# Attention of a hybrid encoder layer: scores of both head pairs and a neighbour's values in one cluster over four PSUM banks

## The chip, the cores and the metric

The kernel runs on one core of one Trainium2 chip. The number is the device time of one launch in microseconds (us). Of a core's engines five matter: TensorE multiplies (in the profile PE, its weight loads PEld), VectorE (DVE), ScalarE (ACT) and GpSimd (POOL) work on elements, and the sync engine (SP) issues most DMAs. TensorE takes its products in the order of the program, and writes them to PSUM, which has eight banks of 512 fp32 columns.

## The reference

One step of a streaming encoder: 2048 prompt positions and 8 x 16 sample positions, model width 1024, two layers. Each layer computes one wide projection of the normed input, two mixers side by side, an output projection, and a gated embedding:

```
u = rms_norm(h) @ w_in ;  qa,ka,va,ga,qb,kb,vb,gb,ab = split(u)
A = window attention(qa, ka, va)   8 heads of 64, 2 key heads, with sinks
    s = q k^T / 8 over the own chunk of 64 keys and the two before (192 keys)
    m = max(max(s), sink) ; pr = exp(s - m) ; den = sum(pr) + exp(sink - m)
    o = (pr / den) v
B = gated linear attention(qb, kb, vb, gates)   4 heads, state 64 x 128 handed on
h = h + [A * silu(ga) ; head_norm(B) * silu(gb)] @ w_out
h = h + sigmoid(rms_norm(h) @ w_pg) * (p @ w_pe)
```

## The kernel before

**Tiles and groups.** The 2176 positions are 17 tiles of 128: 16 of the prompt and one of the sample. `GROUPS` cuts them into groups of 3, 4, 4, 3 and 3 tiles; the last one holds two prompt tiles and the sample tile. For each layer and group `phase_in` makes the projections and both mixers, and `phase_out` the output projection and the gated embedding.

**Big products.** Weights are split into a high and a low part by ACT and DVE (`w_split`), and `mm3` makes three fp32r products for each of 8 blocks of 128 rows: 24 products a unit, over 512 columns or as many as the group has positions (384 or 512). `unit_a` and `unit_b` are such units. They run on the array as one 128*128 tile.

**Small products.** Attention and GLA are fp32 products on parts of the array. Scores use 64 rows (one key head) by 128 columns, two heads' groups side by side; value products use 128 rows by 64 columns for the two full key blocks and 64 by 64 for the halves; GLA scores use 64 by 32. A profile row shows that as 64\*128, 128\*64 and so on, and each fp32 product as two rows. `chain` (L121) strings the products of one cluster together, so that no big product is put between them. `wait_for` adds a wait on the last of them.

**What sets the order.** `pump` (L276) steps generators in the background, in two lanes (`lanes=2`); the units of big products call it behind themselves, those of `vb` and `gb` also in their middle. Each `yield` ends a step. Then a scheduler places the instructions of each engine by estimated times.

**Attention of a prompt tile** (`attn_prompt`, L627). For each of the two head pairs `hp`: four score products into the two banks of `pair("s")`, `softmax` (L581: DVE takes the maximum, ACT four exponentials, DVE scales P), a step later six transposes of P to PSUM, copied by ACT (`ptf`) and DVE (`pth`). When both pairs are through and the gates `ga` are made, the value products go to the two banks of `pair("o")`, and `gate_mix` multiplies them by the gates. A tile's scores of the second pair come one or more steps after the first, with big products between.

**GLA.** `gla_a` makes exponentials and the GLA scores (`at`, `ke`), `gla_prompt` the outputs, the state and the normed output `on`, which `gla_out` transposes. The list of jobs puts `gla_a(0)` in front of the last attention tile; `later` holds the GLA jobs until the projections for them are made. `gla_sample` (group 4 only) makes the state products of the sample from `km` (POOL); `km` and `on` come from the same two buffers (tag `on`).

Of the kernel before, what the change touches and what calls it, by code (L numbers as in the profile page):

```python
# [8 lines left out]
F32 = mybir.dt.float32  # L9
# [37 lines left out]
def hybrid_step(ctx: ExitStack, tc: tile.TileContext, a: dict, o: dict):  # L47
# [84 lines left out]

    def pt(shape):
# [312 lines left out]

    def unit_a(xt, w, m, s0, sn, ps=None, gate=None, ks=(0, KD), end=False):
        c = slice(m * 128, m * 128 + 128)
        mm3(ps, gate=gate, first=ks[0] == 0, last=ks[1] == KD, after=freed(w, 1, ks[0]) if end else None,
            sides=[(w(0, k, c), w(1, k, c), xt[k // 4][:, k % 4, 0, s0:s0 + sn], xt[k // 4][:, k % 4, 1, s0:s0 + sn])  # L450
                   for k in range(*ks)])
        return ps


    def phase_in(l, gi, ip, xn, mslot, S_in):
# [19 lines left out]
        def is_sample(t):  # L475
            return t == NP
# [103 lines left out]
        banks_as("p")  # L580
        done = dict(attn=0, ga=False, S=S_in, g2={}, seq=0, scores=0, qk=False)  # L581
        lock = set()

        def softmax(ps, P, nsink4, wd_of):

# [3 lines left out]
            if wd_of is None:  # L589
                V.tensor_reduce(out=mv, in_=ps, axis=AX.X, op=ALU.max)  # L590
            else:
                for c in range(2):
                    V.tensor_reduce(out=mv[:, :, c], in_=ps[:, :, c, :wd_of[c]], axis=AX.X, op=ALU.max)
            V.scalar_tensor_tensor(out=mv, in0=mv, scalar=-0.125, in1=nsink4, op0=ALU.mult, op1=ALU.min)  # L594
            V.tensor_tensor(out=den[:, 1].rearrange("p (i c) -> p i c", c=2), in0=mv, in1=nsink4, op=ALU.subtract)
            for e in range(4):
                wd = ps.shape[3] if wd_of is None else wd_of[e % 2]
                p0 = 0 if wd_of is None else 128 - 64 * (e % 2)
                A.activation(out=P[:, e, p0:p0 + wd], in_=ps[:, e // 2, e % 2, :wd], func=ACTF.Exp, scale=0.125,  # L599
                             bias=mx[:, e:e + 1], accum_out=den[:, 0, e:e + 1])  # L600
            A.activation(out=den[:, 1], in_=den[:, 1], func=ACTF.Exp)
# [4 lines left out]
            for c in range(2):  # L606
# [21 lines left out]
        def attn_prompt(ti):  # L628
# [60 lines left out]
            done["attn"] += 1  # L689

        def attn_sample(ti):
            ckT = ip.tile([128, 8, 128], F32, tag="E", name="ckT", bufs=2)
# [60 lines left out]
        def later(f):  # L753
            while not done["qk"]:
                yield
            yield from f()
# [3 lines left out]
        order = list(range(nt))  # L760
        jobs = [attn_sample(ti) if is_sample(t) else attn_prompt(ti) for ti, t in aorder]
        if not is_sample(tiles[-1]):
# [10 lines left out]
        for b in range(2):  # L773
            w = w_get(l, gi, f"ga{b}")
            for m in range(2):
                for si, (s0, sn) in enumerate(subs):
                    w_ahead(1, (m + 1 + Z["wah"]) / 2)
                    ps = unit_a(xt, w, m, s0, sn, pm(sn), end=m == 1)
                    sg = sga[:, 2 * b + m, s0:s0 + sn]
# [3 lines left out]
                    if late:  # L783
                        continue
                    pump(Z["pga"])
        done["ga"] = True


        for b, nm in enumerate(("qb", "kb")):
            w = w_get(l, gi, nm)  # L790
            for m in range(2):
                for si, (s0, sn) in enumerate(subs):
                    w_ahead(1, (m + 1 + Z["wah"]) / 2)
                    ps = unit_a(xt, w, m, s0, sn, pm(sn), end=m == 1)
                    dst = qkb[:, b, s0 // TT:(s0 + sn) // TT, m, :]
# [69 lines left out]
        def gla_scores(ti, E):  # L865
# [124 lines left out]
        def gla_sample(ti, sgb):  # L990
# [418 lines left out]
```

## Time and profile before

| | us |
|---|---|
| median of 3 runs (2299.15 to 2301.09) | 2299.72 |
| the profiled execution | 2299.65 |
| its span, first to last instruction | 2297.9 |
| TensorE busy, of the span | 2260.0 (98%) |
| DVE, ACT, POOL busy | 1510.8, 1187.7, 649.6 |

Matmuls are pipelined, and a row's duration reaches from the start of a product to its end, so that rows overlap: the distance between two starts is what a product takes from the stream. The granted clock of TensorE is full (0.995 over the span).

### The profile page before, as it was taken

Reading aid. Unit: us, or ns where it says so; the run is one execution under the profiler, and the core shown is the slowest. Engines: PE = TensorE matmul, PEld = TensorE weight load, DVE = VectorE, ACT = ScalarE, POOL = GpSimd, SP = SyncE. Lnnn points to the kernel's source line nnn. Section 1 sums busy time; section 2 is a strip of 40 time slices with the busy share of each in tenths; the row PEclk is TensorE's granted clock in tenths of the full one; section 3 lists DMA queues with packets and bytes.
Section 4 is the critical chain, followed back from the end, with each engine's and each line's share of the span. In section 5 each row is a group of like instructions: output and inputs, shape, how many; then the busy total and the mean of one; then the engine's idle time right before and its main releaser. Section 6 shows DMA issues by size and latency. Waiting matters only on the chain.

```text
span 2297.9 us, 40325 instructions
## 1 busy us (share of the span) xinstructions
PE 2260.0 (98%) x14814; PEld 1949.3 (85%) x14814; DVE 1510.8 (66%) x3119; ACT 1187.7 (52%) x2802; POOL 649.6 (28%) x771
## 2 busy tenths in 40 slices
PE   8999999999999999999999999999999999999999
PEld 7889877887788889987988998778877888799889
DVE  7767656766567666765776776557665676676655
ACT  6556444654455545644665564445544455565443
POOL 3124212342223221422332241214412142223222
PEclk8999999999999999999999999999999999999999
DMA  5744423434243535553565544234431545365443
GB/s 170 266 150 141 166 87 125 140 111 174 65 157 119 195 107 176 172 194 121 184 208 196 171 133 156 100 122 138 142 142 57 160 126 206 97 188 194 157 137 102
DMA packets 151590, 341.81 MB, mean 149 GB/s; under 512 B 16688, under 2 KB 42672, under 8 KB 138592
## 3 DMA queue, kind: packets, MB, share of 16 engines
q1 hardware_dynamic: 150704, 338.34, 44.8%
q8 instruction: 117, 1.92, 0.3%
q10 hardware_dynamic: 688, 0.88, 0.1%
q14 instruction: 81, 0.66, 0.1%
HBM read 297.35 MB, written 41.68 MB: 148 GB/s over the span
## 4 chain that ended last, share of the span: by engine, by line
PE 84%; ACT 4%; DVE 4%; DMA 4%; issue 3%; POOL 2%; ACTq 0%; DVEq 0%; POOLq 0%; SPq 0%
PE mm L421 15%; PE mm L419 15%; PE mm L420 15%; PE pw L419 9%; PE pw L421 9%; PE pw L420 9%; PE o L131 3%; DMA raw<-in_w_pe_dram 2%; PE s L131 2%; DVE w L96 2%; PE s L125 2%; PE o L125 1%; ACT gsq L914 1%; ACT w L234 1%; PE t L131 1%
## 5 line engine op out<-in xcount | busy, mean ns | idle before, releaser
L96 DVE TENSOR_TENSOR w<-raw,w 128x512 fp32r<-128x512 f32 (+1 forms) x640 | 464.5, 753 | 153.0 <-ACT w L234 151.4
L234 ACT ACTIVATE w<-raw 128x512 fp32r<-128x512 f32 (+1 forms) x640 | 375.4, 627 | 219.3 <-DMA raw<-in_w_pe_dram 60.2
L96 POOL TENSOR_TENSOR ot<-gth,hst 128x384 f32<-128x384 f32 (+1 forms) x79 | 101.7, 1291 | 285.6 <-DVE gth L1208 261.4
L419 PE MATMUL mm<-B,w 128*128 128x384 f32 (+1 forms) x440 | 159.3, 362 | 2.1 <-DVE yq L489 1.5
L421 PE MATMUL mm<-B,w 128*128 128x384 f32 (+1 forms) x440 | 160.2, 364 | 0.0
L420 PE MATMUL mm<-B,w 128*128 128x384 f32 (+1 forms) x440 | 158.8, 361 | 0.0
L419 PE MATMUL pw<-mix,w 128*128 128x384 f32 (+1 forms) x424 | 152.6, 360 | 0.0
L421 PE MATMUL pw<-mix,w 128*128 128x384 f32 (+1 forms) x424 | 151.1, 356 | 0.0
L420 PE MATMUL pw<-mix,w 128*128 128x384 f32 (+1 forms) x424 | 151.0, 356 | 0.0
L420 PE MATMUL mm<-A,w 128*128 128x384 f32 (+1 forms) x408 | 147.9, 363 | 0.0
L419 PE MATMUL mm<-A,w 128*128 128x384 f32 (+1 forms) x408 | 147.4, 361 | 0.0
L421 PE MATMUL mm<-A,w 128*128 128x384 f32 (+1 forms) x408 | 147.4, 362 | 0.0
L96 POOL TENSOR_TENSOR acc<-sq,acc 128x384 f32<-128x384 f32 (+1 forms) x60 | 73.9, 1231 | 258.7 <-ACT sq L350 243.7
L599 ACT ACTIVATE P<-s,mx 128x192 f32<-128x192 f32 (+3 forms) x272 | 108.6, 412 | 71.6 <-DVE mx L594 58.7
L419 PE MATMUL mm<-w,B 128*128 128x512 f32 (+1 forms) x360 | 138.6, 385 | 0.0
L419 PE MATMUL mm<-w,A 128*128 128x512 f32 (+1 forms) x360 | 138.5, 385 | 0.0
L420 PE MATMUL mm<-w,B 128*128 128x512 f32 (+1 forms) x360 | 138.0, 383 | 0.0
L420 PE MATMUL mm<-w,A 128*128 128x512 f32 (+1 forms) x360 | 137.6, 382 | 0.0
L421 PE MATMUL mm<-w,A 128*128 128x512 f32 (+1 forms) x360 | 137.3, 382 | 0.0
L421 PE MATMUL mm<-w,B 128*128 128x512 f32 (+1 forms) x360 | 137.1, 382 | 0.0
L96 POOL TENSOR_TENSOR mix<-ga_t,mix 128x512 fp32r<-128x512 f32 x34 | 44.0, 1295 | 262.9 <-ACT mix L625 262.9
L1205 ACT ACTIVATE gth<-gth 128x384 f32<-128x384 f32 (+2 forms) x81 | 45.1, 560 | 126.0 <-DVE gth L1204 125.7
(325 smaller groups left out, 6337.7 us busy)
## 6 DMA issues: line engine op xcount, KB each, us to landing
raw<-in_w_in_dram SPq DMA_DIRECT2D x240, 256.0 KB, 3.1
raw<-in_w_out_dram SPq DMA_DIRECT2D x160, 256.0 KB, 3.1
raw<-in_w_pg_dram SPq DMA_DIRECT2D x160, 256.0 KB, 3.0
w<-k0vb SPq DMA_DIRECT2D x16, 1024.0 KB, 4.8
w<-k1vb SPq DMA_DIRECT2D x16, 1024.0 KB, 4.8
raw<-in_w_in_dram SPq DMA_DIRECT2D x40, 272.0 KB, 3.0
raw<-in_w_pe_dram SPq DMA_DIRECT2D x40, 256.0 KB, 3.5
w<-k0ga SPq DMA_DIRECT2D x8, 1024.0 KB, 5.4
```

What stands on the lines that cost most here:

```text
L96: (eng or G).tensor_tensor(out=out, in0=in0, in1=in1, op=op1)
L125: prev[0] = PE.matmul(**kw).ins
L131: prev[0] = PE.matmul(**kw).ins
L234: A.activation(out=hi, in_=r, func=ACTF.Copy)
L419: PE.matmul(out=out, lhsT=sh, rhs=mh, start=first and i == 0, stop=False)
L420: PE.matmul(out=out, lhsT=sh, rhs=ml, start=False, stop=False)
L421: lastmm[0] = PE.matmul(out=out, lhsT=sl, rhs=mh, start=False, stop=last and i == n).ins
L599: A.activation(out=P[:, e, p0:p0 + wd], in_=ps[:, e // 2, e % 2, :wd], func=ACTF.Exp, scale=0.125, bias=mx[:, e:e + 1], accum_out=den[:, 0 ...
L914: A.activation(out=gq, in_=po[:, h % 2, h // 2, :], func=ACTF.Square, accum_out=ss[:, h:h + 1])
L1205: ta = A.activation(out=th[:, c], in_=th[:, c], func=ACTF.Tanh, scale=0.5)
```

## The change

A new generator `attn_chain` takes the place of the `attn_prompt` jobs in groups 0 to 3; group 4 keeps the old ones. For each tile it takes four banks (both pairs) and issues one cluster: if the gates are made, first the value products of an earlier tile, into columns 384 to 511 of the four banks in pieces of 128 columns, then the scores of both head pairs into columns 0 to 383. The first product of the cluster waits for all readers of the cluster before; each reader waits for the cluster's last product. Two steps later the transposes of both pairs follow. The values of the last two tiles are issued at the end into one pair. The units of `ga`, `qb` and `kb` now give one step in their middle and one behind, instead of two behind. The GLA jobs start when the last scores are issued. Every `chain` whose products aren't marked `loose` is issued behind the one before it, GLA's too.

```diff
-    def chain(prev, after=(), behind=None, **kw):
+    def chain(prev, after=(), loose=False, **kw):
 
         if prev[0] is None:
-            with tc.issue_after(behind) if behind is not None else ExitStack():
+            with tc.issue_after(clus[0]) if clus[0] is not None and not loose else ExitStack():
...
+        if not loose:
+            clus[0] = prev[0]
+
+    clus = [None]
...
-    def unit_a(xt, w, m, s0, sn, ps=None, gate=None, ks=(0, KD), end=False):
+    def unit_a(xt, w, m, s0, sn, ps=None, gate=None, ks=(0, KD), end=False, mid=None):
         c = slice(m * 128, m * 128 + 128)
-        mm3(ps, gate=gate, first=ks[0] == 0, last=ks[1] == KD, after=freed(w, 1, ks[0]) if end else None,
+        rel = freed(w, 1, ks[0]) if end else None
+
+        def after(i):
+            if rel is not None:
+                rel(i)
+            if mid is not None and i == 3:
+                mid()
...
+                x = V.tensor_reduce(out=mv, in_=ps, axis=AX.X, op=ALU.max)
+                if last is not None:
+                    wait_for(x.ins, last)
...
+            return ex.ins
...
+        def attn_values(job, ots, pv):
+
+            ti, ptf, pth, deps = job
+            first = tiles[ti] == 0
+            w = 256 // len(ots)
+            for c in range(2):
+                half = not (first and c == 1)
+                for x, ot in enumerate(ots):
+                    for g in range(2):
+                        gs = slice(g * 64, g * 64 + 64)
+                        if not (first and c == 0):
+                            chain(pv, deps, out=ot[gs, c], lhsT=vT[:, ti + c, gs], rhs=ptf[:, c, g, x * w:x * w + w], start=True, stop=not half)
+            for x, ot in enumerate(ots):
+                for c in range(2):
+                    full = not (first and c == 0)
+                    hr = slice(c * 64, c * 64 + 64)
+                    for g in range(2):
+                        gs = slice(g * 64, g * 64 + 64)
+                        if not (first and c == 1):
+                            chain(pv, out=ot[gs, c], lhsT=vT[hr, ti + 1 - c, gs], rhs=pth[hr, g, x * w:x * w + w], start=not full, stop=True)
+
+        def gate_mix2(ots, ti, last):
+            tmp = ip.tile([128, 4, 128], F32, tag="ga_t", name="ga_t", bufs=Z["th"])
+            s = slice(ti * TT, ti * TT + TT)
+            tv = tmp.rearrange("p j (c i) -> p j c i", c=2)
+            sv = sga[:, :, s].rearrange("p j (c i) -> p j c i", c=2)
+            m = 4 // len(ots)
+            for x, ot in enumerate(ots):
+                for c in range(2) if m == 4 else (slice(0, 2),):
+                    j = slice(x * m, x * m + m)
+                    in0 = ot[:, c].rearrange("p (j i) -> p j i", j=m) if m == 4 else ot.rearrange("p c (j i) -> p j c i", j=m)
+                    op = V.tensor_tensor(out=tv[:, j, c], in0=in0, in1=sv[:, j, c], op=ALU.mult)
+                    wait_for(op.ins, last)
+            done["readers"].append(op.ins)
+            A.activation(out=mix0[:, :, 0, s], in_=tmp, func=ACTF.Copy)
+            ptt(mix0[:, :, 1, s], tmp, mix0[:, :, 0, s], ALU.subtract)
+            done["attn"] += 1
+
+        def attn_chain(tis):
+
+            kk = kT.rearrange("p s c -> p (s c)")
+            jobs = deque()
+            for ti in tis:
+                first = tiles[ti] == 0
+                while len(jobs) > 1 and not done["ga"]:
+                    yield
+                banks2 = [pair("s"), pair("o")]
+                pv = [None]
+                job = jobs.popleft() if jobs and done["ga"] else None
+
+                busy, done["readers"] = done["readers"], []
+                if job is not None:
+                    job[3].extend(busy)
+                    ots = [b[:, :, 384:512] for b in banks2]
+                    attn_values(job, ots, pv)
+                ls = []
+                for hp in range(2):
+                    lst = banks2[hp][:, :, :384].rearrange("p g (c k) -> p g c k", c=2)
+                    ls.append(lst)
+                    for c in range(2):
+                        k0 = ti * 128 + 64 * c
+                        wd = 192
+                        if first:
+                            k0, wd = 128, 64 + 64 * c
+                        for g in range(2):
+                            gs = slice(g * 64, g * 64 + 64)
+                            chain(pv, busy, out=lst[:, g, c, :wd], lhsT=qT[gs, ti, c * 256 + hp * 128:c * 256 + hp * 128 + 128],
+                                  rhs=kk[gs, k0:k0 + wd], start=True, stop=True)
+                Ps = []
+                for hp in range(2):
+                    P = ip.tile([128, 4, 192], F32, tag="P", name="P", bufs=2)
+                    sink = nsink[:, l, hp:4:2].unsqueeze(2).to_broadcast([128, 2, 2])
+                    done["readers"].append(softmax(ls[hp], P, sink, [64, 128] if first else None, pv[0]))
+                    Ps.append(P)
+                if job is not None:
+                    gate_mix2(ots, job[0], pv[0])
+                if ti == tis[-1]:
+                    done["lastqk"] = True
+                    bg.extend(gjobs)
+                for _ in range(2):
+                    yield
+                ptf = ip.tile([128, 2, 2, 256], F32, tag="ptf", name="ptf", bufs=2)
+                pth = ip.tile([128, 2, 256], F32, tag="pth", name="pth", bufs=2)
+                deps = []
+                for hp in range(2):
+                    deps += turned(ti, hp, Ps[hp], ptf, pth)
+                jobs.append((ti, ptf, pth, deps))
+                for _ in range(1):
+                    yield
+            while not done["ga"] or "o" in lock:
+                yield
+            b = pair("o")
+            pv = [None]
+            last = []
+            for x, job in enumerate(jobs):
+                attn_values(job, [b[:, :, 256 * x:256 * x + 256]], pv)
+            for x, job in enumerate(jobs):
+                gate_mix2([b[:, :, 256 * x:256 * x + 256]], job[0], pv[0])
...
-            while not done["qk"]:
+            while not (done["qk"] and done["lastqk"]):
...
-            jobs[-1:] = [later(lambda: gla_a(0)), jobs[-1], later(lambda: gla_a(1)), later(lambda: gla_b(0, sgbs)),
+            jobs = [attn_chain(list(range(nt)))]
+            gjobs = [later(lambda: gla_a(0)), later(lambda: gla_a(1)), later(lambda: gla_b(0, sgbs)),
                          later(lambda: gla_b(1, sgbs))] + [later(lambda ti=ti: gla(ti, sgbs)) for ti in order[2:]]
         bg.extend(jobs)
+        half = 0 if is_sample(tiles[-1]) else 1
...
-                    ps = unit_a(xt, w, m, s0, sn, pm(sn), end=m == 1)
+                    ps = unit_a(xt, w, m, s0, sn, pm(sn), end=m == 1, mid=lambda: pump(half))
...
-                    pump(Z["pqk"])
+                    pump(Z["pqk"] - half)
...
-                        chain(pv, (done["e3"],), done.get("po"), out=pa[q, e, hp, k], lhsT=E[hs, 1, hp, q], rhs=E[hs, 0, hp, k], start=True, stop=True)
+                        chain(pv, (done["e3"],), out=pa[q, e, hp, k], lhsT=E[hs, 1, hp, q], rhs=E[hs, 0, hp, k], start=True, stop=True)
...
-                        chain(pv, out=pu[hs, b, hp, :], lhsT=km[:, h * 64:h * 64 + 64], rhs=vt[:, h * 128:h * 128 + 128],
+                        chain(pv, loose=True, out=pu[hs, b, hp, :], lhsT=km[:, h * 64:h * 64 + 64], rhs=vt[:, h * 128:h * 128 + 128],
                               start=True, stop=True)
```

TensorE's order in the second group of layer 0 (four tiles). Before, the second tile's first score pair (`s_3131`; `mm` is the unit of big products around it, `t` the transposes of a pair's P):

```order
L419 MATMUL mm_3168<-B1_2082,w_2929 128x512
L420 MATMUL mm_3168<-B1_2082,w_2929 128x512
L125 MATMUL s_3131<-kT_2526,qs_2531 128x192
L131 MATMUL s_3131<-kT_2526,qs_2531 128x192 x3
L421 MATMUL mm_3168<-B1_2082,w_2929 128x512
L656 MATMUL t_3091<-cst_72,P_3029 128x128
```

After, the third tile: the values of the first one (`ptf`, `pth`), then both score pairs, in the banks `s_3238` and `o_3239`, between transposes of the second tile's P:

```order
L425 MATMUL mm_3225<-B1_2084,w_3059 128x512
L125 MATMUL s_3238<-ptf_3079,vT_2529 64x128
L131 MATMUL s_3238<-ptf_3079,vT_2529 64x128
L131 MATMUL o_3239<-ptf_3079,vT_2529 64x128 x2
L131 MATMUL s_3238<-ptf_3079,vT_2529 64x128 x2
L131 MATMUL o_3239<-ptf_3079,vT_2529 64x128 x2
L131 MATMUL s_3238<-pth_3080,vT_2529 64x128 x4
L131 MATMUL o_3239<-pth_3080,vT_2529 64x128 x4
L131 MATMUL s_3238<-kT_2528,qs_2533 128x192 x4
L131 MATMUL o_3239<-kT_2528,qs_2533 128x192 x4
L715 MATMUL t_3195<-cst_72,P_3138 128x128
```

The two score pairs stand in one piece, behind the values, whose products have 128 columns where they had 256.

The end of the same group's input half: the last GLA scores `s_4055` end with two transposes, and the big products of the output projection follow (`mm_4199`, then 12 products `mm_4212`, then `on` transposed and the GLA products `o`). Before:

```order
L894 MATMUL s_4055<-cst_72,E_4006 128x128 x2
L419 MATMUL mm_4199<-mix0_2532,w_3776 128x512
L420 MATMUL mm_4199<-mix0_2532,w_3776 128x512
L421 MATMUL mm_4199<-mix0_2532,w_3776 128x512
L419 MATMUL mm_4212<-mix0_2532,w_3776 128x512
L420 MATMUL mm_4212<-mix0_2532,w_3776 128x512
L421 MATMUL mm_4212<-mix0_2532,w_3776 128x512
```

After (`s_4070`, `mm_4214`, `mm_4227`):

```order
L1032 MATMUL s_4070<-cst_72,E_4021 128x128 x2
L424 MATMUL mm_4214<-mix0_2534,w_3805 128x512
L425 MATMUL mm_4214<-mix0_2534,w_3805 128x512
L423 MATMUL mm_4214<-mix0_2534,w_3805 128x512
L424 MATMUL mm_4214<-mix0_2534,w_3805 128x512
L425 MATMUL mm_4214<-mix0_2534,w_3805 128x512
L423 MATMUL mm_4227<-mix0_2534,w_3805 128x512
```

Five products of the first unit are left behind the scores instead of three; the 12 of the second unit and what follows are the same.

The end of group 4 of layer 0: the last of the sample's state products (`t` from `vb` and `km`, eight for each of four pieces) before, where the piece in front of this one (`t_11013`) stands 21 big products earlier and 16 more follow until `on` is transposed:

```order
L420 MATMUL mm_11148<-w_10858,A1_9293 128x512
L131 MATMUL t_11048<-vb_10646,km_11049 64x128 x4
L131 MATMUL t_11048<-vb_10646,km_11055 64x128 x4
L421 MATMUL mm_11148<-w_10858,A1_9293 128x512
L419 MATMUL mm_11148<-w_10858,A1_9293 128x512
L420 MATMUL mm_11148<-w_10858,A1_9293 128x512
```

After, the last two pieces (`t_11047`, `t_11082`), the transposes of `on` and the sample's GLA output:

```order
L424 MATMUL mm_11296<-mix0_9777,w_10907 128x384
L131 MATMUL t_11047<-vb_10680,km_11048 64x128 x4
L425 MATMUL mm_11296<-mix0_9777,w_10907 128x384
L131 MATMUL t_11047<-vb_10680,km_11054 64x128 x4
L131 MATMUL t_11082<-vb_10680,km_11083 64x128 x4
L131 MATMUL t_11082<-vb_10680,km_11089 64x128 x4
L1069 MATMUL t_11214<-cst_72,on_11126 128x128 x3
L131 MATMUL o_11131<-vb_10680,ats_10740 128x128 x4
L131 MATMUL o_11131<-s0_10955,Em_10695 32x128 x16
L131 MATMUL o_11131<-s0_10957,Em_10695 32x128 x16
```

The last two pieces stand next to each other, directly in front of the transposes of `on`.

## Rows read from the trace of the kernel before

**Rows 1.** The page: span, busy time of each engine.

```profile
span 2297.9 us, 40325 instructions
PE 2260.0 (98%) x14814; PEld 1949.3 (85%) x14814; DVE 1510.8 (66%) x3119; ACT 1187.7 (52%) x2802; POOL 649.6 (28%) x771
```

**Rows 2.** TensorE's waits: what waited <- for what: us, times, longest.

```profile
PE t L931 <- DVE on L920: 6.2, 9, 1.9
...
PE o L125 <- ACT ke L907: 2.9, 4, 0.8
...
PE s L125 <- ACT qs L567: 2.0, 2, 1.7
...
PE o L125 <- DVE on L920: 0.8, 1, 0.8
```

**Rows 3.** Timeline of TensorE, a score pair alone: start, duration, instruction.

```profile
83.65 0.33 PE L420 MATMUL mm<-A,w 128*128 128x384 f32 x1
...
84.00 0.34 PE L419 MATMUL mm<-A,w 128*128 128x384 f32 x1
...
84.53 0.32 PE L125 MATMUL s<-kT,qs 64*128 64x192 f32 x1
84.54 0.65 PE L131 MATMUL s<-kT,qs 64*128 64x192 f32 x5
...
85.40 0.34 PE L421 MATMUL mm<-A,w 128*128 128x384 f32 x1
```

**Rows 4.** Timeline of TensorE around values followed by a score pair.

```profile
334.14 0.39 PE L419 MATMUL mm<-w,B 128*128 128x512 f32 x1
...
336.92 0.50 PE L420 MATMUL mm<-w,B 128*128 128x512 f32 x1
337.26 0.40 PE L421 MATMUL mm<-w,B 128*128 128x512 f32 x1
```

**Rows 5.** Timeline of TensorE: a weight load of values; products of 128 columns.

```profile
117.98 0.13 PEld L125 LDWEIGHTS o<-ptf,vT 128*64 128x64 f32 x1 [0.35 <-issue]
...
126.58 0.66 PE L131 MATMUL t<-vb,ke 128*64 128x128 f32 x8
...
1068.80 1.09 PE L131 MATMUL t<-vb,km 128*64 128x128 f32 x16
```

**Rows 6.** Timeline of TensorE, DVE and ACT, end of a four-tile group.

```profile
386.09 0.39 PE L420 MATMUL mm<-mix,w 128*128 128x512 f32 x1
...
387.00 0.40 PE L421 MATMUL mm<-mix,w 128*128 128x512 f32 x1
...
388.54 0.46 PE L125 MATMUL o<-vb,at 128*128 128x128 f32 x2 [0.71 <-ACT ke L907]
...
387.26 0.72 DVE L904 COPY_PREDICATED at<-mk,s 128x512 f32<-128x512 uint8 x1
...
388.01 0.38 ACT L907 ACTIVATE ke<-s 128x256 f32<-128x256 f32 x1 [2.79 <-DVE at L904]
```

**Rows 7.** Timeline of POOL and DVE in the sample's group.

```profile
1064.07 0.93 POOL L1006 TENSOR_SCALAR km<-ke,cst 128x256 f32<-128x256 f32 x1 [0.16 <-POOL km L1006]
...
1069.56 1.12 DVE L920 SCALAR_TENSOR_TENSOR on<-o,gss,sgb 128x128 f32<-128x128 f32 x4 [0.51 <-issue]
```

**Rows 8.** Timeline of TensorE, ACT and DVE: from scores to P, twice.

```profile
276.75 0.65 PE L131 MATMUL s<-kT,qs 64*128 64x192 f32 x5
...
278.83 0.42 ACT L599 ACTIVATE P<-s,mx 128x192 f32<-128x192 f32 x1
...
281.58 0.96 DVE L609 SCALAR_TENSOR_TENSOR P<-P,den 128x768 f32<-128x768 f32 x1
...
1229.12 0.65 PE L131 MATMUL s<-kT,qs 64*128 64x192 f32 x5
...
1237.47 0.96 DVE L609 SCALAR_TENSOR_TENSOR P<-P,den 128x768 f32<-128x768 f32 x1
```

More of the change, by code (lines that the diff above doesn't have):

```diff
@@ L445, in unit_b @@
         return ps
-    def unit_a(xt, w, m, s0, sn, ps=None, gate=None, ks=(0, KD), end=False):
+    def unit_a(xt, w, m, s0, sn, ps=None, gate=None, ks=(0, KD), end=False, mid=None):
         c = slice(m * 128, m * 128 + 128)
-        mm3(ps, gate=gate, first=ks[0] == 0, last=ks[1] == KD, after=freed(w, 1, ks[0]) if end else None,
+        rel = freed(w, 1, ks[0]) if end else None
[4 more added lines that the diff above has]
+                mid()
+        mm3(ps, gate=gate, first=ks[0] == 0, last=ks[1] == KD, after=after,
             sides=[(w(0, k, c), w(1, k, c), xt[k // 4][:, k % 4, 0, s0:s0 + sn], xt[k // 4][:, k % 4, 1, s0:s0 + sn])
@@ L580, in phase_in, with softmax @@
         banks_as("p")
-        done = dict(attn=0, ga=False, S=S_in, g2={}, seq=0, scores=0, qk=False)
+        done = dict(attn=0, ga=False, S=S_in, g2={}, seq=0, scores=0, qk=False, lastqk=False, readers=[])
         lock = set()
-        def softmax(ps, P, nsink4, wd_of):
+        def softmax(ps, P, nsink4, wd_of, last=None):
             mx = ip.tile([128, 4], F32, tag="mx", name="mx", bufs=2)
@@ L589, in softmax @@
             if wd_of is None:
-                V.tensor_reduce(out=mv, in_=ps, axis=AX.X, op=ALU.max)
+                x = V.tensor_reduce(out=mv, in_=ps, axis=AX.X, op=ALU.max)
+                if last is not None:
+                    wait_for(x.ins, last)
             else:
                 for c in range(2):
-                    V.tensor_reduce(out=mv[:, :, c], in_=ps[:, :, c, :wd_of[c]], axis=AX.X, op=ALU.max)
+                    x = V.tensor_reduce(out=mv[:, :, c], in_=ps[:, :, c, :wd_of[c]], axis=AX.X, op=ALU.max)
+                    if last is not None:
+                        wait_for(x.ins, last)
             V.scalar_tensor_tensor(out=mv, in0=mv, scalar=-0.125, in1=nsink4, op0=ALU.mult, op1=ALU.min)
@@ L598, in softmax @@
                 p0 = 0 if wd_of is None else 128 - 64 * (e % 2)
-                A.activation(out=P[:, e, p0:p0 + wd], in_=ps[:, e // 2, e % 2, :wd], func=ACTF.Exp, scale=0.125,
-                             bias=mx[:, e:e + 1], accum_out=den[:, 0, e:e + 1])
+                ex = A.activation(out=P[:, e, p0:p0 + wd], in_=ps[:, e // 2, e % 2, :wd], func=ACTF.Exp, scale=0.125,
+                                  bias=mx[:, e:e + 1], accum_out=den[:, 0, e:e + 1])
             A.activation(out=den[:, 1], in_=den[:, 1], func=ACTF.Exp)
@@ L689, in attn_prompt, with turned @@
             done["attn"] += 1
+        def turned(ti, hp, P, ptf, pth):
+            first = tiles[ti] == 0
+            pf = pt([128, 2, 2, 128])
+            ph = pt([128, 2, 128])
+            for g in range(2):
+                Pc = P[:, 2 * g:2 * g + 2, :].rearrange("p c k -> p (c k)")
+                if not first:
+                    PE.transpose(out=pf[:, 0, g, :], in_=Pc[:, 0:128], identity=ident)
+                PE.transpose(out=pf[:, 1, g, :], in_=Pc[:, 256:384], identity=ident)
+                m = 64 if first else 128
+                PE.transpose(out=ph[0:m, g, :], in_=Pc[:, 128:128 + m], identity=ident)
+            h = slice(hp * 128, hp * 128 + 128)
+            if first:
+                x = A.activation(out=ptf[:, 1, :, h], in_=pf[:, 1], func=ACTF.Copy).ins
+            else:
+                x = A.activation(out=ptf[:, :, :, h].rearrange("p c g r -> p (c g) r"), in_=pf.rearrange("p c g r -> p (c g) r"), func=ACTF.Copy).ins
+            hs = slice(0, 64) if first else slice(0, 128)
+            return [x, V.tensor_copy(pth[hs, :, h], ph[hs]).ins]
@@ new lines, in attn_chain @@
+        def attn_chain(tis):
+            kk = kT.rearrange("p s c -> p (s c)")
+            jobs = deque()
+            for ti in tis:
+                first = tiles[ti] == 0
+                while len(jobs) > 1 and not done["ga"]:
[15 more added lines that the diff above has]
+                        wd = 192
+                        if first:
+                            k0, wd = 128, 64 + 64 * c
+                        for g in range(2):
+                            gs = slice(g * 64, g * 64 + 64)
[31 more added lines that the diff above has]
+                gate_mix2([b[:, :, 256 * x:256 * x + 256]], job[0], pv[0])
@@ L777, in phase_in @@
                     w_ahead(1, (m + 1 + Z["wah"]) / 2)
-                    ps = unit_a(xt, w, m, s0, sn, pm(sn), end=m == 1)
+                    ps = unit_a(xt, w, m, s0, sn, pm(sn), end=m == 1, mid=lambda: None if late else pump(half))
                     sg = sga[:, 2 * b + m, s0:s0 + sn]
@@ L784, in phase_in @@
                         continue
-                    pump(Z["pga"])
+                    pump(Z["pga"] - half)
         done["ga"] = True
@@ L793, in phase_in @@
                     w_ahead(1, (m + 1 + Z["wah"]) / 2)
-                    ps = unit_a(xt, w, m, s0, sn, pm(sn), end=m == 1)
+                    ps = unit_a(xt, w, m, s0, sn, pm(sn), end=m == 1, mid=lambda: pump(half))
                     dst = qkb[:, b, s0 // TT:(s0 + sn) // TT, m, :]
```

1 line of the change is left out of this document (added).

## The prediction

> **What bounds the kernel now.** I read the totals of the engines first [rows 1]: TensorE's matmul row is busy for 98% of a span of 2297.9 us, and the sum below is made against that execution's own 2299.65 us (0.07 under the median of the three timed runs, 2299.72; the 1.7 us beside the span are the same before and after). Next come the waits of TensorE [rows 2]. The three largest that can concern this change are the transposes of the normed GLA output `on` (6.2 us in 9 waits), the GLA products `o` that wait for `ke` (2.9 us in 4), and `s`, the first scores of a group, that wait for `qT` (2.0 in 2). No row names a product that waits for a softmax. So DVE, ACT and the DMAs lie beside TensorE almost everywhere, and a change is worth what it does to TensorE's own stream: columns streamed, and what a switch between kinds of products costs. The third view is therefore the timeline of TensorE around the small products.
>
> **A score pair by itself** [rows 3]. The starts at 83.65 and 84.00 are two big products of 384 columns apart, 0.35 us. Between the start at 84.00 and that of the second big product behind the scores (85.40) pass 1.40 us; less 0.35 for the two big products, the scores cost 1.05. Their work: each of the four score products is two fp32 passes, and the two heads' groups run side by side on the two halves of the rows, so four slots; the row of five passes (0.65 us, one pass 0.32) holds two slot distances, 0.33, so 0.165 a slot and 0.66 for four. The other 0.39 us is what it costs to go to products of another tile size and back: the array's first starts after each switch come late.
>
> **Values and scores in one stretch** [rows 4]. From the big product at 334.14 to the second one behind (337.26) are 3.12 us, less two big products of 512 columns (0.91 us for four distances between 386.09 and 387.00 [rows 6], so 0.46) 2.66. Work: 6 slots of 256 columns at 0.165 x 256/192 = 0.22, 1.32, and 0.66 for the scores, 1.98. Four changes of tile size (to 128*64, to 64*64, to 64*128, back) share the 0.68 left: 0.17 each. The lone pair gives 0.39/2 = 0.195. So a change of tile size costs 0.17 to 0.195 us of TensorE, whatever its direction.
>
> **The change part by part.**
>
> 1. *Both score pairs together.* Groups 0 to 3 of each layer hold 14 prompt tiles, 28 in all; group 4, with the sample tile, keeps its old attention. Before, each tile goes to 64*128 products twice, after once: counted over the whole order of TensorE, visits to that tile size fall from 96 to 68, exactly 28. A second pair behind the first costs 0.66 instead of 1.05. By the price per change it is 2 x 0.17, so 0.34 to 0.39 each; 28 x 0.37, the middle, = 10.4 us gained. As a check from the other side: changes of tile size fall from 454 to 397, 57 x 0.17 to 0.195 = 9.7 to 11.1. I take 10.4.
>
> 2. *Values of the earlier tile in front of the scores.* This happens in 12 of the 28 tiles (third tile of three, third and fourth of four); before, 14 values stood directly in front of a score pair. That is already in the count of 57 and is no gain by itself. The last two tiles' values stand apart in the new order, with big products between, so nothing is merged there. The 12 values are cut into products of 128 columns instead of 256: 88 more instructions, the same columns. Such short products keep pace: 8 passes of `t` products with the same 128*64 tile take 0.66 and 16 take 1.09 [rows 5], so 0.11 a pair, which is 0.165 x 128/192. Cost 0; the upper bound is in the second rival.
>
> 3. *Readers wait for the whole cluster; the next cluster waits for all readers.* The maximum over the scores may start only when the last product of the cluster has ended, 0.66 us later for the first pair. The softmax of a pair takes 5.1 us in a quiet stretch (scores end at 276.75 + 0.65 = 277.40, the scaled P at 281.58 + 0.96 = 282.54), 8.7 in a busy one (1229.77 to 1238.43) [rows 8]. Behind it, in TensorE's order, stand the transposes of that P; in the closest place (first group, first tile) they come 46 big products of 0.175 later, 8.0 us, elsewhere some 11 us, and the next cluster 9 us or more. A quiet softmax is covered, in the busy first groups barely. I take 0; nothing shorter than nothing can be gained, as before no product waits for a softmax; the upper end is the first rival.
>
> 4. *Order of the clusters.* Every small cluster is now issued behind the one before it. In the four groups with four tiles the last GLA scores come two big products earlier against the GLA products that wait for `ke` (5 + 12 between them instead of 3 + 12). What is late there is the chain `on`, `at`, `ke`: DVE's `at` starts at 387.26 behind `on`, ACT's `ke` at 388.01, and TensorE, idle for 0.71, goes on at 388.54 [rows 6]. All of that chain starts from the stretch that moves, so the wait falls by 2 x 0.23 = 0.46: four times, 1.8 of the 2.9 us gained (bounds 0 and 2.9). In the first group of layer 0 two more big products and more work lie between the same pair; its one wait of 0.8 [rows 2] goes, and I count 1.0 with what is left of the wait behind it.
>
> 5. *The sample group's end.* The state products of the sample come later, and the last two sets stand right behind each other, where 21 big products lay between before. `km` and `on` share two buffers. So the third `km` can be made only when the first product set has ended: 0.93 on POOL, then its products, then `on` (1.12 on DVE) [rows 7] before TensorE may transpose it. From the end of the first set that is 0.93 + 0.43 for a set of 8 passes (1.09 - 0.66 [rows 5]) + 1.12, and 0.1 for each of three hand-overs (`ke`, begun at 388.01 for 0.38, lets TensorE go on 0.15 later [rows 6]): 2.8 us. TensorE has work for some 1.5 of them (three sets and one big product), in layer 1 for 0.7 more (four big products). Loss 1.3 and 0.6: 1.9 us, bounds 0 and 8 (four `km` in a row and both `on` waited for in each layer).
>
> The sum: -10.4 - 1.8 - 1.0 + 1.9 = -11.3, so 2299.65 - 11.3 = 2288.4 us (2288.35). Its own range: the best ends (11.1 + 2.9 + 1.3 gained, nothing lost) give 2284.4, the smaller price, no gain at the group ends and 1.9 lost 2291.9.
>
> **Rivals.**
>
> *The softmax of two pairs is late, and TensorE, which takes its products in order, stands.* Two softmaxes in one burst put four more exponentials of 0.42 and two more DVE passes of 0.96 behind each other [rows 8], some 3.5 us. If the first pair's P gets no precedence, it is ready 5.1 + 3.5 = 8.6 us after the cluster in quiet stretches, 8.7 + 3.5 = 12.2 in busy ones, against the 8.0 to 11 us above. With 3.8 us lost in each of the six tiles of the two first groups and 0.5 in the other 22, that is +34: 2322. It decides from a mean wait of 0.57 us a tile on ((11.3 + 4.6)/28). Against it: before, one pair had 31 big products, 7 us, in its first place, and no wait for P shows. Chance 0.05.
>
> *The short value products pay for their weights.* If the load of the stationary operand (0.13 us for 64 columns [rows 5]) did not run beside the product before it, each of the six extra slots of the 12 tiles would cost 0.13: 12 x 6 x 0.13 = 9.4, and 2297.8 us. The rows of 16 and 8 passes speak against it: 0.11 a pair leaves no room for a load of 0.13 behind a stream of 0.11. Chance 0.04. The Trainium skill, "TensorE: Matmul & The Clock Gate", section "The mechanism" in its part on packing small matmuls, has the rule that makes this rival: a weight load overlaps running matmuls only where the row group differs, and these value products all use every row. By that rule the time would be 2297.8, by the rows 2288.4; the trace disagrees with it for this form.
>
> *A second pair pays its own start.* It writes two other banks; if half of the 0.39 belonged to the pair and not to the switch, the gain of step 1 is 5.2 and the time 2293.6. For it: only one-pair stretches are seen. Against it: the price per change is the same in stretches with two and with four changes. Chance 0.09.
>
> *The ends give it back.* Tails of the groups unchanged and the sample's end at its upper bound: -10.4 + 8 = 2297.3. Chance 0.08.
>
> **How the numbers follow.** The forecast has 0.74. A difference under 0.2%, 4.6 us, can't be told from no change in this measurement: faster is under 2295.1, slower over 2304.3. Faster: 0.73 of the forecast, 0.08 of the third rival and 0.01 of the last, 0.82. The same: 0.01 + 0.01 + 0.04 + 0.07, and 0.01 of a mild first rival, 0.14. Slower: 0.04. The range from 2283 to 2295 leaves out the first two rivals and most of the last, together about 0.16, and takes in the bounds of steps 1 and 4 and half of that of step 5.
>
> **What would show it.** In the profile after: the passes of both score pairs in one stretch of about 1.05 + 0.66 = 1.71 us net; a full stretch of values and both pairs 2.66 + 0.66 = 3.3; waits of the GLA products for `ke` near 1.1 us in total; a new wait of TensorE for `km` or `on` of 1 to 2 us in group 4 of each layer. It would be wrong if the transposes of P or the new clusters show waits for DVE or ACT, if the second pair takes clearly more than 0.66, or if other waits that the new order makes outweigh step 4.

## The result, and the profile after

Five runs each: 2286.22 us (2283.15 to 2287.69) against 2301.09 (2299.15 to 2304.34) for the kernel before in the same set. The ratio is 0.9934, 95% interval 0.9923 to 0.9945: 14.9 us or 0.66% faster, where 2288.4 was forecast.

The page's totals after, against [rows 1]:

```profile
span 2282.7 us, 40621 instructions
PE 2245.0 (98%) x14990; PEld 1956.7 (86%) x14990; DVE 1490.7 (65%) x3119; ACT 1184.1 (52%) x2802; POOL 654.0 (29%) x771
```

The span is 15.2 us shorter and TensorE's busy time 15.0: the gain lies in its stream, not in its waits. Added up over the trace from the first product on, TensorE's idle pieces of over 0.15 us are 30.5 us after and 30.7 before. What is left of the distances from one start to the next falls by 14.1 us, from 397.8 to 383.7, where at least one of the two products is a small one (called the stretches below), and by 0.9 between two big products (tiles `mm` and `pw`).

The waits of TensorE after (what waited, for what: us, times, longest), against [rows 2]:

```profile
PE t L1069 <- DVE on L1058: 6.3, 6, 1.9
PE mm L528 <- ACT w L238: 4.7, 2, 3.5
...
PE s L125 <- ACT qs L578: 2.3, 2, 1.9
...
PE t L576 <- ACT E L989: 0.9, 1, 0.9
...
PE t L131 <- POOL km L1144: 0.4, 1, 0.4
...
PE o L125 <- ACT ke L1045: 0.3, 1, 0.3
```

The waits for `ke` fall from 2.9 to 0.3 and that of `o` for `on` is gone. A wait for `km` and one of the `yq` transposes for `E` are new. No product waits for a softmax. The 3.5 us for the first weights at the start lie ahead of all that was changed.

TensorE around both pairs of a tile (start, duration, instruction), against [rows 3]:

```profile
276.14 0.39 PE L423 MATMUL mm<-B,w 128*128 128x512 f32 x1
276.46 0.43 PE L125 MATMUL s<-kT,qs 64*128 64x192 f32 x1
...
276.73 0.65 PE L131 MATMUL s<-kT,qs 64*128 64x192 f32 x5
277.21 0.82 PE L131 MATMUL o<-kT,qs 64*128 64x192 f32 x8
277.96 0.33 PE L715 MATMUL t<-cst,P 128*128 128x128 f32 x1
...
278.59 0.48 PE L424 MATMUL mm<-B,w 128*128 128x512 f32 x1
278.90 0.39 PE L425 MATMUL mm<-B,w 128*128 128x512 f32 x1
```

Each pair starts 0.75 us before what follows it (276.46, 277.21, 277.96). From 276.14 to 278.90 are 2.76; less two big products (0.46) and six transposes (0.66) the two pairs cost 1.64 net, where a lone one costs 1.05. The weight loads of the second pair (PEld) begin at 277.05, 0.16 us ahead of its products:

```profile
277.05 0.68 PEld L131 LDWEIGHTS o<-kT,qs 64*128 64x128 f32 x8
```

A full cluster, values and both pairs, against [rows 4]:

```profile
289.71 0.48 PE L425 MATMUL mm<-B,w 128*128 128x512 f32 x1
290.12 0.32 PE L125 MATMUL s<-ptf,vT 128*64 128x128 f32 x1
...
290.39 0.39 PE L131 MATMUL o<-ptf,vT 128*64 128x128 f32 x4
290.61 0.39 PE L131 MATMUL s<-ptf,vT 128*64 128x128 f32 x4
290.83 0.39 PE L131 MATMUL o<-ptf,vT 128*64 128x128 f32 x4
291.15 0.45 PE L131 MATMUL s<-pth,vT 64*64 64x128 f32 x8
291.42 0.40 PE L131 MATMUL o<-pth,vT 64*64 64x128 f32 x8
291.75 0.92 PE L131 MATMUL s<-kT,qs 64*128 64x192 f32 x8
292.50 0.82 PE L131 MATMUL o<-kT,qs 64*128 64x192 f32 x8
293.25 0.33 PE L715 MATMUL t<-cst,P 128*128 128x128 f32 x1
...
294.20 0.40 PE L424 MATMUL mm<-B,w 128*128 128x512 f32 x1
```

From 289.71 to 294.20 are 4.49, less 0.46 and 0.66: 3.37 net (3.3 forecast); in the median of the ten such clusters it is 0.1 less. From its first product to the first transpose are 3.13 us. Before, the cluster of [rows 4], with one pair, took 2.46 from its first product to the big product at 336.92:

```profile
334.46 0.43 PE L125 MATMUL o<-ptf,vT 128*64 128x256 f32 x1
```

So the second pair adds 0.66 us, as forecast, and the cut values nothing. Within one tile size four rows, two slots, take 0.22 (290.39, 290.61, 290.83): 0.11 a slot, as forecast. Where the tile size changes, the step is longer: 0.32 from 290.83 to 291.15, then 0.33 from 291.42 to the scores.

### The profile page after: what moved, and what is told of

Same layout as the page of the kernel before. It is cut to its first block, busy times and chain, and to the rows that moved or that the text cites. A ratio compares the mean times of both kernels' runs of the same rounds, so it can differ in the third digit from the quotient of the medians.

```text
span 2282.7 us, 40621 instructions
## 1 busy us (share of the span) xinstructions
PE 2245.0 (98%) x14990; PEld 1956.7 (86%) x14990; DVE 1490.7 (65%) x3119; ACT 1184.1 (52%) x2802; POOL 654.0 (29%) x771
## 4 chain that ended last, share of the span: by engine, by line
PE 89%; ACT 3%; DMA 2%; DVE 2%; issue 2%; POOL 1%; ACTq 0%; DVEq 0%; POOLq 0%
PE mm L423 16%; PE mm L424 16%; PE mm L425 16%; PE pw L423 9%; PE pw L424 9%; PE pw L425 9%; PE o L131 4%; PE s L131 2%; DMA raw<-in_w_pe_dram 1%; PE t L131 1%; PE s L125 1%; PE t L1069 1%; DVE w L96 1%; POOL xacc L96 1%; PE t L576 1%
## 5 line engine op out<-in xcount | busy, mean ns | idle before, releaser
L991 POOL COPY dec<-E 128x2 f32<-128x2 f32 x32 | 12.5, 390 | 381.4 <-ACT E L989 315.2
L96 POOL TENSOR_TENSOR xacc<-sq,xacc 128x384 f32<-128x384 f32 (+1 forms) x66 | 93.7, 1419 | 20.1 <-ACT sq L354 16.9
```

Source lines behind the costliest of these rows:

```text
L96: (eng or G).tensor_tensor(out=out, in0=in0, in1=in1, op=op1)
L991: G.tensor_copy(dec, E[:, 5, :, 127:128])
```

## Experiments

### One more product in front, or between the pairs

```
+  chain(pv, ..., out=banks2[1][:, 0, 0:64], lhsT=ident, rhs=ident[:, 0:64], ...)
```

The line (its other arguments left out) stands ahead of the cluster in the first kernel, ahead of the second pair in the second.

> The changed kernel with one more product in front of each of the 28 clusters: a 128*128 fp32 product of 64 columns (a block of the identity) into columns that the second pair's scores overwrite. It stands next to big products or transposes of the same tile size, so it adds no change of tile size; by the order of TensorE there are 395 of them (397 in the changed kernel). It is the control for the next run. Both theories: 28 x 0.11 us of work = 3.1, less 2 changes of 0.2 = 0.4: 2286.2 + 2.7 = 2289 us (2287 to 2291).

> The same 28 products, but between the two score pairs of a cluster instead of in front of it. Everything else of the order is kept; changes of tile size rise from 395 to 450. Theory (the price is in the change of tile size, 0.17 to 0.235 us each): 55 x 0.2 = 11 us above the run with the product in front (9.4 to 12.9), so about 2300. Rival (the gain of the changed kernel comes from its order and the waits, and a second pair pays its own start anyway): within 3 us of the control, 2289 to 2292. If a second pair pays half of it: about 5.5 above the control, 2294.5.

In front: 2290.31 us, ratio 0.9957 (0.9943 to 0.9970). Between: 2301.94, ratio 1.0006 (0.9997 to 1.0015). The same 28 products cost 4 us in front and 15.7 between. The difference, 11.6 us (about 3.7 either way), is 0.21 for each of the 55 changes of tile size; with the products' own 4 us it eats the whole gain of the change. The timelines show where. In front (first run), then between:

```profile
277.36 0.40 PE L423 MATMUL mm<-B,w 128*128 128x512 f32 x1
...
279.98 0.49 PE L424 MATMUL mm<-B,w 128*128 128x512 f32 x1
```

```profile
279.32 0.39 PE L423 MATMUL mm<-B,w 128*128 128x512 f32 x1
279.64 0.43 PE L125 MATMUL s<-kT,qs 64*128 64x192 f32 x1
...
279.91 0.65 PE L131 MATMUL s<-kT,qs 64*128 64x192 f32 x5
280.49 0.43 PE L131 MATMUL o<-cst 128*128 128x64 f32 x2
280.86 0.92 PE L131 MATMUL o<-kT,qs 64*128 64x192 f32 x8
281.71 0.33 PE L715 MATMUL t<-cst,P 128*128 128x128 f32 x1
...
282.34 0.48 PE L424 MATMUL mm<-B,w 128*128 128x512 f32 x1
...
280.49 0.30 PEld L131 LDWEIGHTS o<-cst 128*128 128x128 f32 x2 [0.23 <-issue]
280.86 0.63 PEld L131 LDWEIGHTS o<-kT,qs 64*128 64x128 f32 x8
```

From the first score to the first transpose are 2.07 us instead of 1.50. From the last big product in front of the cluster to the first behind it are 3.02 us (279.32 to 282.34), with the product in front 2.62 (277.36 to 279.98), in the changed kernel 2.45 (276.14 to 278.59). So the product itself costs 0.17 and the two changes 0.40. The clusters with values show the same: 4.64, 4.25 and 4.07 in the median. In 28 clusters that is 11 us.

The weight loads point to what a change consists of. With the product between, the loads of the second pair begin with its products (280.86) and not 0.16 us ahead, and in front of the product between no load runs for 0.23. Over the trace of the changed kernel a load starts 0.17 us ahead of its product in the median, at a change of tile size together with it (0.00). That the change costs just this lead is likely by these rows; no run takes the two apart.

The theory of the price per change holds, for the scores' tile; the two rivals for it (the order alone; half of the price on the pair) fall.

### The order rule alone, and the change without it

In the kernel before, `chain` gets the line of the changed kernel (with `loose`, which goes with it); in the other run the changed kernel gets the line of before, and with it the old rule that holds the GLA scores alone.

```
-            with tc.issue_after(behind) if behind is not None else ExitStack():
+            with tc.issue_after(clus[0]) if clus[0] is not None and not loose else ExitStack():
```

> The kernel before with only one part of the change: each small cluster is issued behind the last product of the one before it (state products of the sample excepted). Attention per tile, banks and pump calls stay those of before; changes of tile size are 452 against 454. The sample's last state products stand in the order of the changed kernel. Theory: 2 x 0.2 = 0.4 for the changes, 2.0 of the waits for ke gone, 1.0 to 2.0 lost at the sample's end: 2301.1 - 1 = 2300 us (2297 to 2302.5). Rival (the order brings the gain): 2287 to 2292.

> The changed kernel with the order rule of before: only the GLA scores are held behind the GLA products, the other clusters are placed by estimated times. Clusters of both pairs, values in front and the mid pumps stay. Changes of tile size are 424 against 397 and 454, and the sample's end is that of before. Theory: 30 changes fewer than before, 30 x 0.2 = 6.0 gained (5.1 to 7.1), waits for ke as before or up to 1 us less, nothing lost at the sample's end: 2295 us (2293 to 2297). Rival (the order brings the gain): 2299 to 2303, like before.

Order alone: 2361.11 us, ratio 1.0265 (1.0251 to 1.0279), 60 us slower. Neither theory had that. Idle time of TensorE is 67.2 us instead of 30.7, and the stretches cost 422.0 instead of 397.8; the granted clock over the span is 0.984 instead of 0.995. One of the four-tile group ends in its timeline, and the two windows over it (us, then busy of PE, PEld, DVE, ACT, POOL; granted clock; DMA):

```profile
369.27 0.40 PE L425 MATMUL mm<-w,B 128*128 128x512 f32 x1
372.13 0.45 PE L660 MATMUL t<-cst,P 128*128 128x128 f32 x1 [2.46 <-ACT gsq L918]
...
376.54 0.90 PE L935 MATMUL t<-cst,on 128*128 128x128 f32 x3 [2.89 <-DVE on L924]
```

```profile
370.00:376.00 6.00, 1.51 (x6) 1.14 (x6) 3.82 (x9) 4.12 (x13) 5.31 (x8) 0.61 0.00 0
376.00:382.00 6.00, 4.89 (x23) 2.45 (x24) 2.65 (x8) 0.73 (x2) 0.03 (x2) 0.50 0.01 3
```

The last tile's P stands between GLA clusters: its transposes wait 2.46 us behind the squares `gsq` on ACT, and its values can't be issued before the transposes of `on`, which wait 2.89. Behind these gaps the granted clock is 0.50, the lower level of 1.2 GHz, and the products that follow take twice their time (the transposes of P behind the first gap start 0.21 us apart, elsewhere 0.11).

The change with the old order: 2292.87 us, ratio 0.9968 (0.9957 to 0.9979), 8.2 faster than before and 6.7 slower than the full change. The rival falls; the theory's 2295 (2293 to 2297) was 2 us too high. Without the rule, three places mix two clusters product by product. One of them:

```profile
100.36 0.65 PE L131 MATMUL o<-ptf,vT 128*64 128x256 f32 x2
100.94 0.30 PE L131 MATMUL s<-E 64*32 64x64 f32 x2
101.16 0.65 PE L131 MATMUL o<-ptf,vT 128*64 128x256 f32 x2
101.74 0.30 PE L131 MATMUL s<-E 64*32 64x64 f32 x2
...
103.34 0.50 PE L131 MATMUL s<-E 64*32 64x64 f32 x32
```

A value product and a GLA score take 0.80 together; the four value products and three scores from 100.36 to 103.34 take 2.98. With the two groups side by side on the array, four value products take 4 x 0.22 = 0.9. So this place loses some 2.1, and the second one, in layer 1, the same. In the third, halves of values and transposes of `E` mix too: it takes 6.30 (1465.98 to 1472.28), where the same products in the changed kernel take 2.65 (331.61 to 334.26). Together that is some 7.8 by this estimate, and 6.7 by the times, about 3.5 either way. In the changed kernel that is what the rule brings: clusters stay whole. The price is paid twice there: all 12 additional visits to the 64\*32 tile and 9 of the 10 to 128\*64 stand in these places, and the two groups' products no longer share the array.

### Why the rule alone costs 60 us

First the GLA jobs were put behind the attention:

```
-            jobs[-1:] = [later(lambda: gla_a(0)), jobs[-1], later(lambda: gla_a(1)), ...
+            jobs += [later(lambda: gla_a(0)), later(lambda: gla_a(1)), ...
```

> The kernel before with the order rule (each small cluster behind the one before it), which alone gave 2361, and with the job of the first GLA scores moved behind the last attention tile. Nothing is merged; changes of tile size are 448. Theory (the 60 us came from the last attention tile standing between GLA clusters: transposes of P behind the squares on ACT, values behind the bank pair of the GLA outputs, and the clock at its lower level, 0.50, behind these gaps): nearly all of it goes, 2303 us (2298 to 2309). Rival (a fixed order of the small clusters costs that by itself, wherever the GLA jobs stand): over 2330.

2363.24 us, ratio 1.0270 (1.0256 to 1.0284): my theory fell, and the time was what the rival allowed. The waits moved. No P waits any more; now the GLA tail does, here at the end of the same group (TensorE, ACT, POOL, DVE):

```profile
384.44 0.66 PE L131 MATMUL t<-vb,ke 128*64 128x128 f32 x8
...
395.06 1.16 PE L935 MATMUL t<-cst,on 128*128 128x128 f32 x4 [5.39 <-DVE on L924]
...
390.06 0.28 ACT L918 ACTIVATE gsq<-o 128x128 f32<-128x128 f32 x1
...
393.51 1.01 POOL L921 TENSOR_TENSOR gss<-gss,mhalf 128x4 f32<-128x4 f32 x1
...
394.56 1.12 DVE L924 SCALAR_TENSOR_TENSOR on<-o,gss,sgb 128x128 f32<-128x128 f32 x4 [2.60 <-POOL gss L921]
```

The chain from the GLA products over the squares, the power on POOL and `on` takes 10.6 us (384.44 to 395.06), since the next tile's exponentials and products share ACT, DVE and POOL with it. In TensorE's order only 12 big products, 2.7 us, stand beside it; in the changed kernel 38 do. From that I argued that the attention ended too late in the group: each score pair uses the one bank pair of tag `s` and, with the order fixed, holds up all behind it until its softmax has read the banks. The next run gave the second pair the other banks and changed nothing else:

```
-                lst = pair("s")[:, :, :384]...
+                lst = pair("so"[hp])[:, :, :384]...
```

> The kernel with the order rule and the GLA jobs behind the attention (2363), and one thing more: the second score pair of a tile takes the other two banks, so that it needn't wait until the first pair's softmax has read its banks. Nothing is merged by that. Now the GLA clusters at the end of a four-tile group have 37, 34, 13 and 12 big products between them instead of 33, 12, 12 and 12, in a three-tile group mostly 24, 12 and 12 instead of 11, 12 and 12. Theory (under the order rule the end of a group waits because the attention is through too late, one pair of banks at a time, and the GLA chain of 10.6 us from products to on has only 12 big products beside it): the four waits of 5.4 to 5.9 us of the four-tile groups shrink to under 2 each, some 2 us go in each three-tile group, and with the clock that falls behind them and 13 x 0.2 for changes it is 2363 - 16 - 10 - 8 - 3 = 2326 us (2310 to 2338). Rival (a fixed order of unmerged clusters costs the 60 us by itself): 2350 to 2363.

2303.73 us, ratio 1.0015 (1.0005 to 1.0024): 59.5 us came back, 22 more than forecast, so the rival that both runs share (a fixed order costs this by itself) falls; idle time is 35.8 and the stretches 397.1. At the end of a four-tile group a wait like this is left:

```profile
648.73 0.46 PE L125 MATMUL o<-vb,at 128*128 128x128 f32 x2 [1.11 <-DVE on L924]
```

So of the 62 us that the run before cost, 59.5 hang on the second pair's having banks of its own; some 2.6 of them would be the 13 changes of tile size that also went. The run with the rule alone, whose waits lie elsewhere, wasn't repeated with two bank pairs. The changed kernel takes four banks for each cluster, and waits like these don't show in it.

### The ends: km, and the last values

```
+                km2 = ip.tile([128, 2, 256], F32, tag="on", name="km", bufs=2)
...
-                    km = ip.tile([128, 256], F32, tag="on", name="km", bufs=2)
+                    km = km2[:, b]
```

> The changed kernel with the two km tiles of a set (1 KB each, each in a 2 KB buffer of tag on) put together into one buffer, so that a set takes one of the two buffers instead of both. The last two sets then stand in one stretch; changes of tile size are 391 against 397. Theory of step 5 (the sample's end loses 1 to 2 us a run because km and on share buffers): the wait for km (0.4) goes, and the end of the sample group gains 1.0 to 1.9 besides 6 x 0.21 = 1.3 for the changes: 2283.0 us (2282 to 2284). Rival (the end is set by the chain from the last GLA outputs over the squares, gss and on to the transposes, 4.0 us against 12 big products of 0.175 = 2.1, and the waits of 1.86, 0.93, 1.86 and 1.20 stay): only 1.3 + 0.4, 2284.5.

2285.84 us, ratio 0.9929 (0.9917 to 0.9942), above the theory's range: no difference from the changed kernel that these runs can tell, also not the 1.3 for six changes. The trace decides: of the waits in the sample's group that for `km` is gone, those for `on` stay (1.80 and 0.74 in layer 0, 1.84 and 1.17 in layer 1, against 1.86, 0.93, 1.86, 1.20):

```profile
1061.36 1.97 PE L131 MATMUL t<-vb,km 128*64 128x128 f32 x32
...
1072.47 1.02 PE L1069 MATMUL t<-cst,on 128*128 128x128 f32 x4 [1.80 <-DVE on L1058]
1080.22 1.01 PE L1069 MATMUL t<-cst,on 128*128 128x128 f32 x4 [0.74 <-DVE on L1058]
```

So the shared buffers don't make these waits. That the chain behind the last GLA products makes them, as the rival has it, fits; no run shortened that chain.

Then the values of a group's last two tiles in one cluster, the second tile with its halves first (the part of `attn_values` that reads the new argument is not shown):

```
+            jobs[0][3].extend(d for job in list(jobs)[1:] for d in job[3])
...
-                attn_values(job, [b[:, :, 256 * x:256 * x + 256]], pv)
+                attn_values(job, [b[:, :, 256 * x:256 * x + 256]], pv, (0, 1) if x == 0 else (1, 0))
```

> The changed kernel with the values of the last two tiles of a group in one cluster: they wait for both tiles' copies of P, and the second tile's halves come in front of its full blocks, so that the cluster goes to 128*64, 64*64, 128*64 and back. Changes of tile size fall from 397 to 379. Theory (0.21 us for each change, whatever its tile sizes): 18 x 0.21 = 3.8 gained, 2282.4 us (2281 to 2284.5), no new wait, since the GLA products that follow stand 25 and 59 big products behind. Rival (the price holds for the scores' 64*128 tile only, or the later values make the GLA tail late): 2286 to 2288.

2280.93 us, ratio 0.9912 (0.9898 to 0.9925): 5.3 under the changed kernel (about 4 either way), against 3.8 for 18 changes at 0.21. The rival falls. No product waits for the later values, and the waits for `on` are 5.2 in all instead of 6.3. The stretches are 4.1 us shorter, 0.23 a change; the rest can't be told from the spread of the runs.

> The changed kernel with both the km pair in one buffer and the last two tiles' values in one cluster; 373 changes of tile size. Theory: 24 x 0.21 = 5.0 and the wait of 0.4: 2280.8 us (2279 to 2283). Rival (neither adds to the other, or the ends give it back): 2283.5 to 2286.

Both edits: 2278.35 us, ratio 0.9901 (0.9886 to 0.9916), 7.9 under the changed kernel and 22.7 under the kernel before: the fastest of all that ran, and just under the forecast range. Beside the last run that is 2.6 for the `km` pair, which alone showed 0.4; the runs don't tell the two apart.

## Why the prediction was right

**What bounds the kernel.** Right: the 15 us came out of TensorE's busy time, and the sum of its idle time did not move. The size was short by a quarter: 14.9 us against 11.3. The stretches and the big products gave 15.0 where 10.4 was counted, and the waits 0.2 where 0.9 was. That 2288.4 lies nearer to 2286.22 than that is luck: the kernel before ran 1.4 us slower in this set than in the execution that the sum started from.

**Step 1, both pairs together.** Right, and the largest term. 28 x 0.37 = 10.4 was forecast. Undone in place it costs 11.6 by the times and 11 by the timelines, so 0.20 to 0.21 a change instead of 0.17 to 0.195. The two pairs took 1.64 net (1.71 forecast), the full cluster 3.37 (3.3), the second pair 0.66 (0.66). For all 57 changes, 0.2 each makes 11.4 of the 14.1 by which the stretches fell. The other 2.7, and the 0.9 in the distances between big products, no run assigns.

**Step 2, values in 128 columns.** Right: 0.11 a slot, no cost. The rival that each weight load is paid for (9.4 us) does not show. Its rule, in the Trainium skill, "TensorE: Matmul & The Clock Gate", section "The mechanism", is that a load overlaps running matmuls only where the row group differs; the trace disagrees with it for products over all rows (0.11 us a slot), as [rows 5] did. The forecast put all six extra slots under it; two of the six are the halves, which use 64 rows.

**Step 3, readers of a whole cluster.** Right: no wait for a softmax or a P after the change. The rival of a late softmax did not come.

**Step 4, order of the clusters.** The waits named went further than forecast: `ke` from 2.9 to 0.3 (1.1 forecast), `o` for `on` from 0.8 to none, so 3.4 gained where 2.8 were counted. Not all of it is the rule's: with the old order `ke` waits 1.8 in all and `o` never for `on`, so the rule brings 1.5 and the rest comes without it. And the idle time as a whole stayed, since the sample's end, the start and one wait for `E` took as much back. The step's view of the rule was too narrow as well. I priced it at the waits that it shortens; the run with the rule alone cost 60 us, and its worth inside the change, 6.7, is in the main that clusters no longer mix. The turn-around of a bank pair under a fixed order stands nowhere in the sum; that it cost nothing here, where the same change took four banks, was luck.

**Step 5, the sample's end.** Right in size, and in part by luck, for the reason was wrong in part. Four waits of 4.73 us became 6.48 (five over 0.15 and two of 0.14 between products), 1.8 more against 1.9 forecast. These are the rows in layer 0:

```profile
1062.63 0.66 PE L131 MATMUL t<-vb,km 128*64 128x128 f32 x8 [0.36 <-POOL km L1144]
...
1071.52 1.01 PE L1069 MATMUL t<-cst,on 128*128 128x128 f32 x4 [1.86 <-DVE on L1058]
```

But the shared buffers of `km` and `on` make only 0.6 of it (0.36 and two of 0.14): the longer waits for `on`, 1.1 more in layer 1, stay when the buffers are no longer shared.

**The rivals.** A second pair that pays its own start: refuted by the product between, and by the 0.66 that the second pair adds. The ends that give it back: they gave back 1.8, far from 8.

## What to carry to other kernels

Where TensorE switches between parts of the array and full products all the time, count the changes of tile size in its order: here each cost 0.2 us where one was put between two score pairs, and merging two clusters saves two of them. For other tile sizes the price is less sure: 18 changes around values came to 0.23 us each by the trace, six around `km` to nothing that shows. Fix the order of such clusters only together with enough PSUM banks: here the fixed order, with the GLA jobs behind the attention, cost 62 us with one bank pair for the scores and 2.8 with two, and the bill came at another place, the end of the group. Price a rule by running it alone; inside a change that also removes its cost it looks free.

## What was not expected of the hardware

Two value products on the two halves of the columns shared the array where they stood next to each other in the order, and not elsewhere: alternated with GLA scores, a product of 256 columns took 0.58 us up to the next start, the change of tile size in it, against 0.22 for its share when side by side. And a gap of 2.5 and one of 2.9 us close together were followed by the clock's lower level (0.50 over the next 6 us); in the 6 us in which the single wait of 5.39 us ended (392 to 398) it was 0.63, in the next 6 us 0.80.
